# Output projection to MLP: the scheduler's order replaced by one written out by hand

## The chip, the core and the metric

The kernel runs on one core of a Trainium2 chip. TensorE (PE in the rows; its weight loads are PEld) multiplies matrices, VectorE (DVE), ScalarE (ACT) and GpSimd (POOL) do the work on elements, and SyncE (SP) issues the transfers from and to memory. Each engine has a queue of its own; semaphores order the engines among each other. The metric is the device time of one execution in microseconds (us), lower is better.

## What is computed

Two layers of a diffusion backbone, for 128 context tokens and 512 latent tokens that share the weights. The kernel keeps all 640 tokens in one array. Each layer ends so:

```python
merged = ga * (oa @ p['w_br_a']) + gb * (ob @ p['w_br_b']) + gc * (oc @ p['w_br_c'])
x = x + g1 * (merged @ p['w_out'])
h2 = _rmsnorm(x, p['norm2']) * (1 + sc2) + sh2
a, g = jnp.split(_dwconv3(h2 @ p['w_up'], p['conv_w'], p['conv_b']), 2, axis=-1)
x = x + g2 * ((jax.nn.silu(a) * g) @ p['w_down'])
```

`x` has 1024 channels, `w_out` is 1024 by 1024, `w_up` 1024 by 5632. `_rmsnorm` divides each token by the root of the mean of its squares over the 1024 channels. The change concerns the three lines in the middle: output projection, norm, first product of the MLP.

## The kernel before

Channels lie on the 128 partitions, tokens along the free axis. `x` is a tile of 128 x 8 x 640: eight channel blocks, 640 tokens. Every 32-bit operand is split into a high and a low part (`split`, L94: ScalarE writes the high part `hi` as a rounded copy, then VectorE the low part `lo` as the difference), and `mm3` (L111) makes a product of three matmuls: low weight by high data, high weight by low data, high by high. In the rows these three stand at L112, L113, L114.

A weight tile is fetched by `load_w` (L98): a transfer into `st` (three buffers), then the split into `wh` by ScalarE and `wl` by VectorE (five buffers of each). Splitting the weights is thus steady work for both engines during every dense stage.

The stretch in question begins at the end of `merge_phase` (L747), which leaves eight tiles `m32[n]`. `out_phase` (L816) splits them into `mh`/`ml` for the two token chunks `CH_B` (tokens 0 to 319 and 320 to 639). Then, for each chunk:

- eight output tiles, n = 0 to 7, of 24 matmuls each (eight channel blocks, three products) in the PSUM tile `wo`; after each, VectorE adds it to `x` with the gate (L837), ScalarE squares the new `x` into `sq` (L165) and the squares are summed in `acc` (class `Acc`: VectorE copies the first and adds the last, GpSimd adds those between);
- `bcast_rstd` (L173) and `rstd_bcast` (L182): TensorE sums `acc` over the partitions (`stat`), VectorE and GpSimd make the reciprocal roots in two pieces (128-wide and 64-wide), VectorE writes three diagonal tiles `dg` and TensorE spreads them over the partitions (`bc2`);
- `modulate` (L200): for each of the eight channel blocks and each token group (the first chunk holds 128 context and 192 latent tokens with different scales, the second only latent ones) VectorE writes `ht`, ScalarE `h2h`, VectorE `h2l`.

`mlp_up` (L848) then makes one `up` tile of `w_up` after another: 24 matmuls on the first chunk and 24 on the second into the two banks of one PSUM tile. There are three such double-bank tiles in PSUM; ScalarE reads each out twice (`u`, L861 and `v`, L862) before it comes free. The 44 `up` tiles of a layer alternate between the two halves of `w_up`.

The order of all this is not that of the code: the kernel is built with a scheduler that gives each engine's instructions an order by its own model of the time, over the whole program. In the program before, it lets `wo` tiles overlap, makes the modulation of the first chunk run between the additions of the second, and takes three `up` tiles through the first chunk before any goes to the second.

Of the kernel before, what the change touches and what calls it, by code (L numbers as in the profile page):

```python
# [27 lines left out]
F_T = 22  # L28
EPS = 1e-6
# [11 lines left out]
CH_B = [(0, 320), (320, 640)]  # L41
# [15 lines left out]
def trunk_kernel(ctx: ExitStack, tc: tile.TileContext, a: dict):  # L57
    nc = tc.nc
    dma = nc.sync.dma_start
    vec, act, pool, pe = nc.vector, nc.scalar, nc.gpsimd, nc.tensor  # L60
# [50 lines left out]
    def mm3(out, sh, sl, mh, ml, start, stop):  # L111
        pe.matmul(out, sl, mh, start=start, stop=False)  # L112
        pe.matmul(out, sh, ml, start=False, stop=False)  # L113
        pe.matmul(out, sh, mh, start=False, stop=stop)  # L114

    def powr(out, x):
        n = x.shape[1]
        pool.tensor_tensor(out=out, in0=x, in1=mhalf[:, :n], op=ALU.pow)
# [54 lines left out]
    def bcast_rstd(pl, sq, w, scale, ps):  # L173

        n = (w + P - 1) // P
        st = ps_t.tile([P, 8], F32, tag="p", name="stat")
        for j in range(n):
            m = min(P, w - j * P)
            pe.matmul(st[:m, j:j + 1], sq[:, j * P:j * P + m], ones[:, 0:1], start=True, stop=True)
        rstd_bcast(pl, st, w, scale, ps)  # L180
# [19 lines left out]
    def modulate(pl, x, bc, A, B, a0, b0, hi, lo):  # L200

        for s, e, j in _segs(a0, b0):
            r = slice(s - a0, e - a0)
            for k in range(ND):
                t = pl.tile([P, 320], F32, tag="ht", name="ht", bufs=3)[:, :e - s]
                vec.scalar_tensor_tensor(out=t, in0=x[:, k, s:e], scalar=A[:, k, j:j + 1], in1=bc[:, r],
                                         op0=ALU.mult, op1=ALU.mult)
                act.activation(hi[:, k, r], t, AF.Identity, bias=B[:, k, j:j + 1])  # L208
                vec.scalar_tensor_tensor(out=lo[:, k, r], in0=t, scalar=B[:, k, j:j + 1],  # L209
                                         in1=hi[:, k, r].bitcast(F32), op0=ALU.add, op1=ALU.subtract)  # L210
# [605 lines left out]
    def out_phase(l, x, rp, m32, hp, ps_d):  # L816

        mh = [hp.tile([P, 8, 320], F32R, tag=f"h{c}", name=f"mh{c}") for c in range(2)]
        ml = [hp.tile([P, 8, 320], F32R, tag=f"l{c}", name=f"ml{c}") for c in range(2)]
        for c, (a0, b0) in enumerate(CH_B):  # L820
            for n in range(8):
                split(m32[n][:, a0:b0], mh[c][:, n], ml[c][:, n], (vec, pool)[c])
        A2 = scale_cols(l, V_N2, 32, "A2")
        B2 = mods[l][:, 24:32, :]
        h2h, h2l = [], []
        for c, (a0, b0) in enumerate(CH_B):
            acc = Acc(rp, 320)
            for n0 in range(0, 8, 2):
                ps = ps_d.tile("wo")
                for j in range(2):  # L830
                    n = n0 + j
                    hi, lo = load_w(a["w_out"][l, n], 1024)
                    for k in range(ND):
                        ks = slice(k * P, (k + 1) * P)
                        mm3(ps[:, j, :320], hi[:, ks], lo[:, ks], mh[c][:, k], ml[c][:, k], k == 0, k == 7)
                    for s, e, jj in _segs(a0, b0):
                        vec.scalar_tensor_tensor(out=x[:, n, s:e], in0=ps[:, j, s - a0:e - a0],  # L837
                                                 scalar=mods[l][:, 16 + n, jj:jj + 1], in1=x[:, n, s:e],
                                                 op0=ALU.mult, op1=ALU.add)
                    acc.add(x[:, n, a0:b0], n == 7)  # L840
            h2h.append(hp.tile([P, 8, 320], F32R, tag=f"h{c}", name=f"h2h{c}"))
            h2l.append(hp.tile([P, 8, 320], F32R, tag=f"l{c}", name=f"h2l{c}"))
            bc = ps_t.tile([P, 512], F32, tag="p", name="bc2")
            bcast_rstd(rp, acc.acc, 320, 1.0 / D, bc)
            modulate(rp, x, bc, A2, B2, a0, b0, h2h[c], h2l[c])
        return h2h, h2l

    def mlp_up(l, f, h2h, h2l, mp, ps_d):  # L848
        vs = []
        for part in range(2):  # L850
            n = part * F_T + f
            hi, lo = load_w(a["w_up"][l, n], 1024)
            ps = ps_d.tile("up")
            for c in range(2):
                for k in range(ND):
                    ks = slice(k * P, (k + 1) * P)
                    mm3(ps[:, c, :320], hi[:, ks], lo[:, ks], h2h[c][:, k], h2l[c][:, k], k == 0, k == 7)
            u = mp.tile([P, T], F32, tag="u", name="u", bufs=2)
            v = mp.tile([P, T], F32, tag="v", name="v", bufs=4)
            cw = [vecs[l][:, V_CW + i * 44 + n:V_CW + i * 44 + n + 1] for i in range(3)]  # L860
            act.activation(u.rearrange("p (c n) -> p c n", c=2), ps[:, :, :320], AF.Copy)  # L861
            act.activation(v.rearrange("p (c n) -> p c n", c=2), ps[:, :, :320], AF.Identity,  # L862
                           bias=vecs[l][:, V_CB + n:V_CB + n + 1], scale=cw[1])
            for s, e in ((0, NP), (NP, T)):
                vec.scalar_tensor_tensor(out=v[:, s + 1:e], in0=u[:, s:e - 1], scalar=cw[0], in1=v[:, s + 1:e],  # L865
                                         op0=ALU.mult, op1=ALU.add)
                vec.scalar_tensor_tensor(out=v[:, s:e - 1], in0=u[:, s + 1:e], scalar=cw[2], in1=v[:, s:e - 1],
                                         op0=ALU.mult, op1=ALU.add)
            vs.append(v)
        va, vg = vs  # L870
        after[0] = vg[:, 0:1]
        act.activation(va, va, AF.Silu)
        vec.tensor_tensor(out=va, in0=va, in1=vg, op=ALU.mult)
        ah = mp.tile([P, T], F32R, tag="ah", name="ah", bufs=8)
        al = mp.tile([P, T], F32R, tag="al", name="al", bufs=8)
        split(va, ah, al)
        return ah, al
# [58 lines left out]
    def h0(a0, b0):  # L936

        j = 0 if a0 < NP else 1
        for k in range(ND):
            t = rp.tile([P, 320], F32, tag="ht", name="ht", bufs=3)[:, :b0 - a0]  # L940
            xs, hi = x[:, k, a0:b0], hh[:, k, a0:b0]
            act.activation(hi, xs, AF.Identity, bias=mods[0][:, k, j:j + 1], scale=A1[:, k, j:j + 1])
            vec.tensor_scalar(out=t, in0=xs, scalar1=A1[:, k, j:j + 1], scalar2=mods[0][:, k, j:j + 1],
                              op0=ALU.mult, op1=ALU.add)
            vec.tensor_tensor(out=hl[:, k, a0:b0], in0=t, in1=hi.bitcast(F32), op=ALU.subtract)
# [26 lines left out]
    for l in range(L):  # L972
# [11 lines left out]
        with ExitStack() as ms:  # L984
            mp = tp("mg", 1, ms)
            cs = modp.tile([P, 2, 1024], F32, tag="cs", name="cs", bufs=1)
            msteps = mod_steps(l, range(2, 6), modp, cs)
            m32 = merge_phase(l, x, cs, hh, hl, mp, ps_d, msteps)
            hst.close()
            hst = ExitStack()  # L990
            hp = tp("h2p", 1, hst, side="right")
            h2h, h2l = out_phase(l, x, rp, m32, hp, ps_d)
        with ExitStack() as ms:
            mp = tp("mlp", 1, ms)
            ups = {}
# [166 lines left out]
```

## Time and profile before

| | us |
|---|---|
| median of three runs | 2300.72 (2298.7 to 2303.47) |
| the profiled execution | 2307.55 |
| its span, first to last instruction | 2305.3 |
| layer 0: first `wo` matmul to first matmul of the fourth `up` tile | 639.65 to 727.05 |
| layer 1: the same | 1769.25 to 1856.66 |

The profiled execution is 6.8 us above the median. Times in rows count from the first instruction; one row is one instruction or several alike in a run (x2, x3). "idle before" is how long the engine had nothing to do, and after the arrow stands what ended it.

### The profile page before, as it was taken

To read this page: it belongs to the slowest core of one execution; us is meant where nothing else is said; L and a number is where in the kernel's file an instruction comes from. 1 tells how busy PE (TensorE), PEld (TensorE's weight loads), DVE (VectorE), ACT (ScalarE), POOL (GpSimd) and SP (SyncE) were. 2 spreads that over 40 slices of the span, in tenths; PEclk is the share of its full clock that TensorE was granted. 3 is DMA by queue.
4 is the path that set the end of the run, shared out by engine and by line. 5 is a ranking of instruction groups with operands and counts; after the bars stand their busy time and mean duration, and the time that the engine had idled before them with its cause. 6 is when DMAs were issued, how large, how long until landed. Compare 5 with 4: busy or idle time off the path is not lost. (4 is left out here: it accounts for less than half of the span.)

```text
span 2305.3 us, 37922 instructions
## 1 busy us (share of the span) xinstructions
PE 2225.9 (97%) x14778; PEld 2163.6 (94%) x14778; DVE 1562.8 (68%) x2913; ACT 975.7 (42%) x1728; POOL 528.4 (23%) x651
## 2 busy tenths in 40 slices
PE   8898999999999999999979999999999999999999
PEld 4898989989999999999969989899999999999999
DVE  6877687559567756765587867864895676554555
ACT  4555555432244423333355645653323453242422
POOL 3753443024041000000047533320422200000000
PEclk8999999999999999999999999999999999999999
DMA  7211223367333333432242112224762332322123
GB/s 256 80 57 59 82 66 107 108 244 228 121 121 106 101 104 121 135 102 88 75 128 83 57 49 83 97 89 135 283 210 89 123 110 92 94 65 90 50 84 114
DMA packets 102775, 258.50 MB, mean 112 GB/s; under 512 B 19523, under 2 KB 32579, under 8 KB 102596
## 3 DMA queue, kind: packets, MB, share of 16 engines
q1 hardware_dynamic: 102596, 256.09, 34.1%
q8 instruction: 116, 1.90, 0.3%
q14 instruction: 63, 0.51, 0.1%
HBM read 233.10 MB, written 22.95 MB: 111 GB/s over the span
## 5 line engine op out<-in xcount | busy, mean ns | idle before, releaser
L95 ACT ACTIVATE wh<-st 128x1024 fp32r<-128x1024 f32 (+3 forms) x336 | 314.7, 943 | 297.0 <-PE dn L114 170.8
L113 PE MATMUL up<-h2l,wh 128*128 128x320 f32 x1408 | 435.6, 310 | 2.5 <-DVE h2l L209 2.4
L112 PE MATMUL up<-h2h,wl 128*128 128x320 f32 x1408 | 433.5, 310 | 2.4 <-ACT v L862 1.4
L114 PE MATMUL up<-h2h,wh 128*128 128x320 f32 x1408 | 435.0, 310 | 0.0
L96 DVE TENSOR_TENSOR wl<-st,wh 128x1024 fp32r<-128x1024 f32 (+3 forms) x336 | 375.4, 1120 | 71.7 <-ACT wh L95 71.1
L113 PEld LDWEIGHTS up<-h2l,wh 128*128 128x128 f32 x1408 | 265.2, 189 | 3.6 <-DVE h2l L209 3.6
L112 PEld LDWEIGHTS up<-h2h,wl 128*128 128x128 f32 x1408 | 264.5, 189 | 4.0 <-ACT h2h L208 2.1
L114 PEld LDWEIGHTS up<-h2h,wh 128*128 128x128 f32 x1408 | 265.3, 189 | 0.1
L143 DVE SCALAR_TENSOR_TENSOR junk<-stm,cs 128x1024 bf16<-128x1024 f32 x172 | 223.2, 1298 | 60.1 <-DMA stm<-in_w_mod 57.2
L865 DVE SCALAR_TENSOR_TENSOR v<-u,vecs,v 128x127 f32<-128x127 f32 (+1 forms) x176 | 89.1, 547 | 183.4 <-ACT v L862 183.4
L112 PE MATMUL mm<-wh,hl 128*128 128x384 f32 x480 | 169.5, 353 | 15.0 <-ACT raw L361 10.8
L113 PE MATMUL dn<-al,wh 128*128 128x320 f32 x544 | 168.1, 309 | 0.0
L114 PE MATMUL dn<-ah,wh 128*128 128x320 f32 x544 | 168.1, 309 | 0.0
L112 PE MATMUL dn<-ah,wl 128*128 128x320 f32 x544 | 168.1, 309 | 0.0
L113 PE MATMUL mm<-wl,hh 128*128 128x384 f32 x480 | 163.7, 341 | 2.6 <-DVE wl L96 2.6
L114 PE MATMUL mm<-wh,hh 128*128 128x384 f32 x480 | 163.4, 340 | 0.0
L114 PE MATMUL gp<-hh,wh 128*128 128x320 f32 x480 | 148.6, 310 | 0.0
L112 PE MATMUL gp<-hh,wl 128*128 128x320 f32 x480 | 148.4, 310 | 0.0
L113 PE MATMUL gp<-hl,wh 128*128 128x320 f32 x480 | 148.3, 309 | 0.0
L112 PE MATMUL mmu<-hh,wl 128*128 128x384 f32 (+1 forms) x416 | 134.0, 322 | 4.0 <-ACT up L677 2.0
L114 PE MATMUL mmu<-hh,wh 128*128 128x384 f32 (+1 forms) x416 | 131.0, 315 | 0.0
L113 PE MATMUL mmu<-hl,wh 128*128 128x384 f32 (+1 forms) x416 | 130.4, 314 | 0.0
(226 smaller groups left out, 5444.6 us busy)
## 6 DMA issues: line engine op xcount, KB each, us to landing
stm<-in_w_mod SPq DMA_DIRECT2D x88, 512.0 KB, 4.3
st<-in_w_up SPq DMA_DIRECT2D x88, 512.0 KB, 3.6
st<-in_w_gate SPq DMA_DIRECT2D x48, 512.0 KB, 4.4
st<-in_w_unit SPq DMA_DIRECT2D x48, 384.0 KB, 3.2
st<-in_w_out SPq DMA_DIRECT2D x32, 512.0 KB, 3.6
st<-in_w_down SPq DMA_DIRECT2D x48, 320.0 KB, 3.0
st<-in_w_br SPq DMA_DIRECT2D x24, 512.0 KB, 3.6
st<-in_w_down SPq DMA_DIRECT2D x32, 384.0 KB, 3.2
```

Source lines behind the costliest of these rows:

```text
L95: act.activation(hi, x, AF.Copy)
L96: eng.tensor_tensor(out=lo, in0=x, in1=hi.bitcast(F32), op=ALU.subtract)
L112: pe.matmul(out, sl, mh, start=start, stop=False)
L113: pe.matmul(out, sh, ml, start=False, stop=False)
L114: pe.matmul(out, sh, mh, start=False, stop=stop)
L143: vec.scalar_tensor_tensor(out=junk, in0=st, scalar=1.0, in1=cs[:, j], op0=ALU.mult, op1=ALU.mult, accum_out=col)
L865: vec.scalar_tensor_tensor(out=v[:, s + 1:e], in0=u[:, s:e - 1], scalar=cw[0], in1=v[:, s + 1:e], op0=ALU.mult, op1=ALU.add)
```

## The change

The scheduler's order for this stretch is replaced: `out_phase` calls a new function `wo_up` inside a section in which each engine keeps the order of the code. Outside it the scheduler works as before.

What the hand-written order does:

- The sixteen `wo` tiles (i = 0 to 15, eight for each chunk) go through TensorE one after another, each complete. After the matmuls of tile i the code issues the load and split of weight tile i + 2, and after that the addition and the square of tile i. The three first `up` weight tiles are numbers 16, 17 and 18.
- The first square of a chunk is written straight into `acc`, with no copy. The sums `stat` are made in three 128-wide pieces at token offsets 0, 128 and 192, so one instruction each makes the mean, the reciprocal root and the diagonals (`dg3`, three at a time), and two matmuls of 256 and 64 columns spread them.
- The sums of the first chunk come after tile 8, their spread after tile 9. Its modulation goes in pieces of one channel block: one piece for each even tile from 10 on, two for each odd one, between the split of weight tile i + 2 and the addition of tile i. The low part of a block comes one piece later than its high part.
- Three `up` tiles then go through the first chunk. The sums of the second chunk stand between the first and the second of them, the spread within the third. The modulation of the second chunk is issued whole, and TensorE takes the three tiles through the second chunk block by block.
- `mlp_up` takes these three from `first` and makes only their readout; `ht` buffers grow from 320 to 384 columns.

```diff
-        for c, (a0, b0) in enumerate(CH_B):
-            acc = Acc(rp, 320)
-            for n0 in range(0, 8, 2):
...
+        with tc.manual_schedule():
+            wo_up(l, x, rp, mh, ml, hp, ps_d, A2, B2, h2h, h2l, first)
...
+            if n == 0:
+                accs.append(rp.tile([P, 384], F32, tag="acc", name="acc", bufs=1))
+                act.activation(accs[c][:, :320], x[:, n, a0:b0], AF.Square)
+                return
...
+        def diag(c):
+            dgs[c] = rp.tile([P, 3, P], F32, tag="ht", name="dg3", bufs=3)
+            vec.tensor_tensor(out=dgs[c], in0=ident.unsqueeze(1).to_broadcast([P, 3, P]),
+                              in1=rrs[c][:, :3].unsqueeze(2).to_broadcast([P, 3, P]), op=ALU.mult)
...
+        def pieces(c):
...
+            for k in range(ND):
+                t = rp.tile([P, 384], F32, tag="ht", name="ht", bufs=3)
...
+                if before is not None:
+                    low(*before)
+                before = k, t
+                yield
+            low(*before)
+            yield
...
+        for i in range(16):
+            c, n = divmod(i, 8)
+            if n % 2 == 0:
+                ps = ps_d.tile("wo")
+            hi, lo = W.pop(i)
+            for k in range(ND):
+                ks = slice(k * P, (k + 1) * P)
+                mm3(ps[:, n % 2, :320], hi[:, ks], lo[:, ks], mh[c][:, k], ml[c][:, k], k == 0, k == 7)
+            load(i + 2)
+            if i == 8:
+                last(0)
+                stat(0)
+            if i == 9:
+                diag(0)
+                spread(0)
+            if i >= 10:
+                p0 = p0 or pieces(0)
+                for _ in range(2 if i % 2 else 1):
+                    next(p0, None)
+            evac(i, ps)
+            if i == 8:
+                rstd(0)
+        u = [ps_d.tile("up")]
+        last(1)
+        for k in range(ND):
+            up(u[0], 16, 0, k)
+        load(18)
+        stat(1)
+        rstd(1)
+        diag(1)
...
+        for k in range(ND):
+            if k == 3:
+                spread(1)
+            up(u[2], 18, 0, k)
+        for _ in pieces(1):
+            pass
+        for k in range(ND):
+            for i in range(3):
+                up(u[i], 16 + i, 1, k)
```

The next rows are TensorE's in layer 0, in the first output tiles: `wo_7190` and `wo_7262` are the PSUM tiles of n = 0 and n = 1 in the program before, `mh0`, `ml0` the split input of the first chunk, whose last channel blocks come from the last tiles of the merge.

```order
L114 MATMUL wo_7190<-mh0_7152,wh_7193 128x320
L112 MATMUL wo_7262<-mh0_7152,wl_7266 128x320
L112 MATMUL wo_7190<-mh0_7152,wl_7194 128x320
L113 MATMUL wo_7262<-ml0_7154,wh_7265 128x320
L114 MATMUL wo_7262<-mh0_7152,wh_7265 128x320
L112 MATMUL wo_7262<-mh0_7152,wl_7266 128x320
L113 MATMUL wo_7262<-ml0_7154,wh_7265 128x320
```

In the changed program the same place reads so; `wo_7204` holds n = 0 and then n = 1 (weights `wh_7194`, then `wh_7200`).

```order
L112 MATMUL wo_7204<-mh0_7152,wl_7195 128x320
L113 MATMUL wo_7204<-ml0_7154,wh_7194 128x320
L114 MATMUL wo_7204<-mh0_7152,wh_7194 128x320
L112 MATMUL wo_7204<-mh0_7152,wl_7201 128x320
L113 MATMUL wo_7204<-ml0_7154,wh_7200 128x320
```

Before, tile n = 1 begins while n = 0 still lacks its last blocks; now n = 0 runs through all eight blocks first.

VectorE before, in the modulation of the first chunk (x is the addition of a `wo` tile, `wl_7899` and `wl_7962` are low parts of weight tiles):

```order
L206 SCALAR_TENSOR_TENSOR ht_7505<-x_5272,A2_7188,bc2_7477 128x128
L837 SCALAR_TENSOR_TENSOR x_5272<-wo_7631,mod0_88,x_5272 128x320
L209 SCALAR_TENSOR_TENSOR h2l0_7476<-ht_7497,mod0_88,h2h0_7475 128x128
L837 SCALAR_TENSOR_TENSOR x_5272<-wo_7700,mod0_88,x_5272 128x320
L209 SCALAR_TENSOR_TENSOR h2l0_7476<-ht_7501,mod0_88,h2h0_7475 128x128
L206 SCALAR_TENSOR_TENSOR ht_7509<-x_5272,A2_7188,bc2_7477 128x128
L96 TENSOR_TENSOR wl_7899<-st_7896,wh_7898 128x1024
L206 SCALAR_TENSOR_TENSOR ht_7513<-x_5272,A2_7188,bc2_7477 128x128
L209 SCALAR_TENSOR_TENSOR h2l0_7476<-ht_7505,mod0_88,h2h0_7475 128x128
L96 TENSOR_TENSOR wl_7962<-st_7959,wh_7961 128x1024
```

VectorE in the changed program, from the low part of weight tile 13 to that of weight tile 14 (`wo_7568` holds tiles 10 and 11; the addition here is that of tile 11):

```order
L96 TENSOR_TENSOR wl_7637<-st_7634,wh_7636 128x1024
L914 SCALAR_TENSOR_TENSOR ht_7640<-x_5272,A2_7188,bc2_7561 128x128
L914 SCALAR_TENSOR_TENSOR ht_7640<-x_5272,A2_7188,bc2_7561 128x192
L907 SCALAR_TENSOR_TENSOR h2l0_7600<-ht_7601,mod0_88,h2h0_7599 128x128
L907 SCALAR_TENSOR_TENSOR h2l0_7600<-ht_7601,mod0_88,h2h0_7599 128x192
L914 SCALAR_TENSOR_TENSOR ht_7647<-x_5272,A2_7188,bc2_7561 128x128
L914 SCALAR_TENSOR_TENSOR ht_7647<-x_5272,A2_7188,bc2_7561 128x192
L907 SCALAR_TENSOR_TENSOR h2l0_7600<-ht_7640,mod0_88,h2h0_7599 128x128
L907 SCALAR_TENSOR_TENSOR h2l0_7600<-ht_7640,mod0_88,h2h0_7599 128x192
L850 SCALAR_TENSOR_TENSOR x_5272<-wo_7568,mod0_88,x_5272 128x320
L96 TENSOR_TENSOR wl_7686<-st_7683,wh_7685 128x1024
```

Two whole channel blocks stand between a weight's low part and the addition, and the addition directly ahead of the next weight's low part.

ScalarE before, over the same stretch (`wh` is a weight's high part, `sq` the square of a new x tile, `h2h0` the high part of the modulated input):

```order
L165 ACTIVATE sq_7663<-x_5272 128x320
L208 ACTIVATE h2h0_7475<-ht_7497,mod0_88 128x128
L208 ACTIVATE h2h0_7475<-ht_7501,mod0_88 128x128
L95 ACTIVATE wh_7898<-st_7896 128x1024
L208 ACTIVATE h2h0_7475<-ht_7505,mod0_88 128x128
L95 ACTIVATE wh_7961<-st_7959 128x1024
L165 ACTIVATE sq_7697<-x_5272 128x320
L165 ACTIVATE sq_7732<-x_5272 128x320
```

ScalarE in the changed program, from the square of tile 10 to the high part of weight tile 14:

```order
L858 ACTIVATE sq_7607<-x_5272 128x320
L95 ACTIVATE wh_7636<-st_7634 128x1024
L918 ACTIVATE h2h0_7599<-ht_7640,mod0_88 128x128
L918 ACTIVATE h2h0_7599<-ht_7640,mod0_88 128x192
L918 ACTIVATE h2h0_7599<-ht_7647,mod0_88 128x128
L918 ACTIVATE h2h0_7599<-ht_7647,mod0_88 128x192
L858 ACTIVATE sq_7655<-x_5272 128x320
L95 ACTIVATE wh_7685<-st_7683 128x1024
```

Every weight's high part now stands directly behind the square of the tile three numbers earlier. Of the rest of the program the order stays, but for the attention of layer 1: there the scheduler, which sees other times ahead, interleaves the same instructions in another order over a stretch of about 1,150 matmul rows.

## Rows read from the trace of the kernel before

**Rows 1.** The page, part 1, TensorE: busy us (share) and instructions.

```profile
PE 2225.9 (97%) x14778; PEld 2163.6 (94%) x14778; DVE 1562.8 (68%) x2913; ACT 975.7 (42%) x1728; POOL 528.4 (23%) x651
```

**Rows 2.** Timeline of TensorE, layer 0: start, us, what.

```profile
639.65 0.31 PE L112 MATMUL wo<-mh,wl 128*128 128x320 f32 x1
...
682.20 0.61 PE L198 MATMUL bc<-dg,ones 128*128 128x128 f32 x4
...
699.36 0.42 PE L113 MATMUL up<-h2l,wh 128*128 128x320 f32 x1 [1.18 <-DVE h2l L209]
...
702.42 0.24 PE L179 MATMUL stat<-ones,acc 128*128 128x1 f32 x1 [0.98 <-DVE acc L171]
...
715.19 0.42 PE L112 MATMUL up<-h2h,wl 128*128 128x320 f32 x1 [0.45 <-ACT h2h L208]
...
727.05 0.41 PE L112 MATMUL up<-h2h,wl 128*128 128x320 f32 x1 [0.69 <-ACT v L862]
```

**Rows 3.** Timeline of TensorE, layer 1.

```profile
1769.25 0.31 PE L112 MATMUL wo<-mh,wl 128*128 128x320 f32 x1
...
1856.66 0.41 PE L112 MATMUL up<-h2h,wl 128*128 128x320 f32 x1 [0.69 <-ACT v L862]
```

**Rows 4.** Timeline of ScalarE, layer 0.

```profile
650.33 0.46 ACT L165 ACTIVATE sq<-x 128x320 f32<-128x320 f32 x1
650.69 1.04 ACT L95 ACTIVATE wh<-st 128x1024 fp32r<-128x1024 f32 x1
...
664.49 1.06 ACT L95 ACTIVATE wh<-st 128x1024 fp32r<-128x1024 f32 x1 [2.10 <-PE wo L114]
...
668.01 1.06 ACT L95 ACTIVATE wh<-st 128x1024 fp32r<-128x1024 f32 x1 [2.10 <-PE wo L114]
...
681.31 0.47 ACT L165 ACTIVATE sq<-x 128x320 f32<-128x320 f32 x1 [0.93 <-DVE x L837]
```

**Rows 5.** Windows, by engine; PEclk is the granted clock.

```profile
core 0: us, PE busy (x) PEld busy (x) DVE busy (x) ACT busy (x) POOL busy (x), PEclk, DMA share, GB/s
698.00:701.00 3.00, 1.75 (x11) 1.31 (x10) 3.00 (x8) 2.12 (x5) 0.83 (x1) 1.00 0.62 187
704.00:707.00 3.00, 3.00 (x13) 3.00 (x13) 2.49 (x9) 1.31 (x4) 1.37 (x2) 0.50 0.21 86
```

**Rows 6.** Timeline of VectorE, end of the merge, layer 0.

```profile
638.96 1.68 DVE L96 TENSOR_TENSOR wl<-st,wh 128x1024 fp32r<-128x1024 f32 x1
...
642.38 1.21 DVE L96 TENSOR_TENSOR wl<-st,wh 128x1024 fp32r<-128x1024 f32 x1
...
645.54 0.55 DVE L96 TENSOR_TENSOR ml<-m,mh 128x320 fp32r<-128x320 f32 x1 [0.54 <-ACT mh L95]
```

**Rows 7.** Timeline of VectorE, additions, modulation, weights, layer 0.

```profile
665.59 1.23 DVE L96 TENSOR_TENSOR wl<-st,wh 128x1024 fp32r<-128x1024 f32 x1 [0.42 <-ACT wh L95]
...
680.68 0.54 DVE L837 SCALAR_TENSOR_TENSOR x<-wo,mod,x 128x320 f32<-128x320 f32 x1
...
692.46 0.33 DVE L206 SCALAR_TENSOR_TENSOR ht<-x,A,bc 128x128 f32<-128x128 f32 x1
692.71 0.34 DVE L209 SCALAR_TENSOR_TENSOR h2l<-ht,mod,h2h 128x128 fp32r<-128x128 f32 x1
...
699.69 1.05 DVE L206 SCALAR_TENSOR_TENSOR ht<-x,A,bc 128x192 f32<-128x192 f32 x3
700.66 1.21 DVE L96 TENSOR_TENSOR wl<-st,wh 128x1024 fp32r<-128x1024 f32 x1
701.80 0.48 DVE L171 TENSOR_TENSOR acc<-acc,sq 128x320 f32<-128x320 f32 x1
```

**Rows 8.** Window in the attention of layer 1.

```profile
1300.00:1350.00 50.00, 43.22 (x261) 40.49 (x260) 42.04 (x102) 25.84 (x63) 17.03 (x30) 0.90 0.17 56
```

**Rows 9.** Waits of TensorE, 1150 to 1560: us, times, longest.

```profile
PE mm L112 <- ACT raw L361: 6.3, 6, 4.1
```

More of the change, by code (lines that the diff above doesn't have):

```diff
@@ L204, in modulate @@
             for k in range(ND):
-                t = pl.tile([P, 320], F32, tag="ht", name="ht", bufs=3)[:, :e - s]
+                t = pl.tile([P, 384], F32, tag="ht", name="ht", bufs=3)[:, :e - s]
                 vec.scalar_tensor_tensor(out=t, in0=x[:, k, s:e], scalar=A[:, k, j:j + 1], in1=bc[:, r],
@@ L824, in out_phase @@
         B2 = mods[l][:, 24:32, :]
-        h2h, h2l = [], []
-        for c, (a0, b0) in enumerate(CH_B):
-            acc = Acc(rp, 320)
-            for n0 in range(0, 8, 2):
-                ps = ps_d.tile("wo")
[L830 to L845, printed above, removed]
@@ L846, in out_phase, with wo_up, load, evac @@
-        return h2h, h2l
-    def mlp_up(l, f, h2h, h2l, mp, ps_d):
+        h2h, h2l, first = [], [], {}
+        with tc.manual_schedule():
+            wo_up(l, x, rp, mh, ml, hp, ps_d, A2, B2, h2h, h2l, first)
+        return h2h, h2l, first
+    def wo_up(l, x, rp, mh, ml, hp, ps_d, A2, B2, h2h, h2l, first):
+        ups = [(0, 0), (1, 0), (0, 1)]
+        W = {}
+        def load(i):
+            if i < 16:
+                W[i] = load_w(a["w_out"][l, i % 8], 1024)
+            elif i < 19:
+                part, f = ups[i - 16]
+                W[i] = load_w(a["w_up"][l, part * F_T + f], 1024)
+        accs, lasts = [], []
+        def evac(i, ps):
+            c, n = divmod(i, 8)
+            a0, b0 = CH_B[c]
+            for s, e, jj in _segs(a0, b0):
+                vec.scalar_tensor_tensor(out=x[:, n, s:e], in0=ps[:, n % 2, s - a0:e - a0],
+                                         scalar=mods[l][:, 16 + n, jj:jj + 1], in1=x[:, n, s:e],
+                                         op0=ALU.mult, op1=ALU.add)
+            if n == 0:
+                accs.append(rp.tile([P, 384], F32, tag="acc", name="acc", bufs=1))
+                act.activation(accs[c][:, :320], x[:, n, a0:b0], AF.Square)
+                return
+            sq = rp.tile([P, 384], F32, tag="sq", name="sq", bufs=2)
+            act.activation(sq[:, :320], x[:, n, a0:b0], AF.Square)
+            if n < 7:
+                pool.tensor_tensor(out=accs[c][:, :320], in0=accs[c][:, :320], in1=sq[:, :320], op=ALU.add)
+            else:
+                lasts.append(sq)
+        def last(c):
+            vec.tensor_tensor(out=accs[c][:, :320], in0=accs[c][:, :320], in1=lasts[c][:, :320], op=ALU.add)
+        OFF = (0, 128, 192)
+        st = {}
+        def stat(c):
+            st[c] = ps_t.tile([P, 8], F32, tag="p", name="stat")
+            for j, o in enumerate(OFF):
+                pe.matmul(st[c][:, j:j + 1], accs[c][:, o:o + P], ones[:, 0:1], start=True, stop=True)
+        rrs, dgs, bcs = {}, {}, {}
+        def rstd(c):
+            ms = small.tile([P, 8], F32, tag="ms", name="ms")
+            rrs[c] = small.tile([P, 8], F32, tag="rr", name="rr")
+            vec.tensor_scalar(out=ms[:, :3], in0=st[c][:, :3], scalar1=1.0 / D, scalar2=EPS,
+                              op0=ALU.mult, op1=ALU.add)
+            powr(rrs[c][:, :3], ms[:, :3])
+        def diag(c):
+            dgs[c] = rp.tile([P, 3, P], F32, tag="ht", name="dg3", bufs=3)
+            vec.tensor_tensor(out=dgs[c], in0=ident.unsqueeze(1).to_broadcast([P, 3, P]),
+                              in1=rrs[c][:, :3].unsqueeze(2).to_broadcast([P, 3, P]), op=ALU.mult)
+        def spread(c):
+            bcs[c] = ps_t.tile([P, 512], F32, tag="p", name="bc2")
+            pe.matmul(bcs[c][:, :256], ones, dgs[c][:, :2].rearrange("p j n -> p (j n)"), start=True, stop=True)
+            pe.matmul(bcs[c][:, 256:320], ones, dgs[c][:, 2, 64:], start=True, stop=True)
+        def pieces(c):
+            a0, b0 = CH_B[c]
+            hi = hp.tile([P, 8, 320], F32R, tag=f"h{c}", name=f"h2h{c}")
+            lo = hp.tile([P, 8, 320], F32R, tag=f"l{c}", name=f"h2l{c}")
+            h2h.append(hi)
+            h2l.append(lo)
+            before = None
+            def low(k, t):
+                for s, e, j in _segs(a0, b0):
+                    r = slice(s - a0, e - a0)
+                    vec.scalar_tensor_tensor(out=lo[:, k, r], in0=t[:, r], scalar=B2[:, k, j:j + 1],
+                                             in1=hi[:, k, r].bitcast(F32), op0=ALU.add, op1=ALU.subtract)
+            for k in range(ND):
+                t = rp.tile([P, 384], F32, tag="ht", name="ht", bufs=3)
+                for s, e, j in _segs(a0, b0):
+                    r = slice(s - a0, e - a0)
+                    vec.scalar_tensor_tensor(out=t[:, r], in0=x[:, k, s:e], scalar=A2[:, k, j:j + 1],
+                                             in1=bcs[c][:, r], op0=ALU.mult, op1=ALU.mult)
+                for s, e, j in _segs(a0, b0):
+                    r = slice(s - a0, e - a0)
+                    act.activation(hi[:, k, r], t[:, r], AF.Identity, bias=B2[:, k, j:j + 1])
+                if before is not None:
[4 more added lines that the diff above has]
+            yield
+        def up(ps, i, c, k):
+            hi, lo = W[i]
+            ks = slice(k * P, (k + 1) * P)
+            mm3(ps[:, c, :320], hi[:, ks], lo[:, ks], h2h[c][:, k], h2l[c][:, k], k == 0, k == 7)
+        load(0)
+        load(1)
+        p0 = None
+        for i in range(16):
+            c, n = divmod(i, 8)
+            if n % 2 == 0:
+                ps = ps_d.tile("wo")
+            hi, lo = W.pop(i)
+            for k in range(ND):
+                ks = slice(k * P, (k + 1) * P)
+                mm3(ps[:, n % 2, :320], hi[:, ks], lo[:, ks], mh[c][:, k], ml[c][:, k], k == 0, k == 7)
[21 more added lines that the diff above has]
+        diag(1)
+        u.append(ps_d.tile("up"))
+        for k in range(ND):
+            up(u[1], 17, 0, k)
+        u.append(ps_d.tile("up"))
+        for k in range(ND):
[4 more added lines that the diff above has]
+            pass
+        for k in range(ND):
+            for i in range(3):
+                up(u[i], 16 + i, 1, k)
+        first.update(zip(ups, u))
@@ L849, in mlp_up @@
+    def mlp_up(l, f, h2h, h2l, first, mp, ps_d):
         vs = []
@@ L851, in mlp_up @@
             n = part * F_T + f
[L852 to L857, printed above, removed]
+            ps = first.pop((part, f), None)
+            if ps is None:
+                hi, lo = load_w(a["w_up"][l, n], 1024)
+                ps = ps_d.tile("up")
+                for c in range(2):
+                    for k in range(ND):
+                        ks = slice(k * P, (k + 1) * P)
+                        mm3(ps[:, c, :320], hi[:, ks], lo[:, ks], h2h[c][:, k], h2l[c][:, k], k == 0, k == 7)
             u = mp.tile([P, T], F32, tag="u", name="u", bufs=2)
@@ L939, in h0 @@
         for k in range(ND):
-            t = rp.tile([P, 320], F32, tag="ht", name="ht", bufs=3)[:, :b0 - a0]
+            t = rp.tile([P, 384], F32, tag="ht", name="ht", bufs=3)[:, :b0 - a0]
             xs, hi = x[:, k, a0:b0], hh[:, k, a0:b0]
@@ L991, in trunk_kernel @@
             hp = tp("h2p", 1, hst, side="right")
-            h2h, h2l = out_phase(l, x, rp, m32, hp, ps_d)
+            h2h, h2l, first = out_phase(l, x, rp, m32, hp, ps_d)
         with ExitStack() as ms:
@@ L1000, in up_to @@
                 for i in range(len(ups), f):
-                    ups[i] = mlp_up(l, i, h2h, h2l, mp, ps_d)
+                    ups[i] = mlp_up(l, i, h2h, h2l, first, mp, ps_d)
                     for _ in range(1 if i < GROUPS[0][1] + 2 else 2):
```

## The prediction

> **What bounds the kernel now.** I read the page first: TensorE is busy 97% of the span [rows 1]. So the stretch can only gain where TensorE waits, runs at half clock or does small matmuls, and it loses whatever new wait the order puts in front of it. Then I read TensorE's timeline from the first `wo` matmul to the first matmul of the fourth `up` tile, which the edit does not own but which must follow it: 639.65 to 727.05, 87.40 us in layer 0, and 1769.25 to 1856.66, 87.41, in layer 1 [rows 2, 3]. The layers agree, so one sum serves both.
>
> What would it be without waits? ScalarE begins successive weight tiles at 664.49 and 668.01, both released by the end of a `wo` tile [rows 4]: TensorE takes 3.52 us for a tile of 24 matmuls, 0.1467 us each. The stretch has 16 `wo` tiles and three `up` tiles of two halves, 22 × 3.52 = 77.44 us. The excess is 9.96 us a layer. The timeline gives 1.18 (low part of the modulated input), 0.98 (`acc` for the sums), 0.45 (high part) and 0.69 (PSUM of the fourth `up` tile) as waits, 3.30 together [rows 2]. [...]
>
> Third, the queues. VectorE is busy all 3.00 us of 698 to 701, while TensorE has 1.75 [rows 5]. What it does there and when it may do it decides this change.
>
> **The change, part by part.** I follow VectorE, since in the new order its queue has one fixed loop from tile 10 on: low part of a weight (`wl`), one or two modulation pieces, addition of a tile (`x`), next `wl`.
>
> *The loop.* `wl` of tile i + 3 needs `wh` of that tile, which stands on ScalarE directly behind the square of tile i, which needs the addition of tile i. The rows price this chain: addition to square 0.63 (680.68 on VectorE, 681.31 on ScalarE), square to the next `wh` 0.36 (650.33 to 650.69), `wh` to `wl` 1.10 (664.49 to 665.59) [rows 4, 7]. That is 2.09 us from addition to `wl`, of which VectorE works only some 0.5. `wl` itself holds the queue 1.14 (700.66 to 701.80). A piece for one channel block is `ht` 0.25 (128 wide, 692.46 to 692.71), 0.32 (192 wide, a third of 699.69 to 700.66), and the two low parts, which I estimate 0.03 to 0.05 above those, 0.30 and 0.35: 1.22 us [rows 7]. One turn is then 2.09 + 1.14 + 1.22 = 4.45 with one piece and 5.67 with two. TensorE wants 3.52. Without the 1.5 us in which VectorE stands idle a turn, two turns would be 2 × 1.14 + 2 × 0.55 + 3 × 1.22 = 7.0 against TensorE's 7.04: the work fits, the order doesn't.
>
> Counted from the addition of tile 10, those of 11 to 15 come at 5.7, 10.1, 15.8, 20.2 and 25.3 us (in the last turn the low part of the seventh block stands in place of a piece's first half). TensorE ends tile 15 about 17.4 us after that addition. `wo` tiles don't stop for it, since their weights run two ahead and their PSUM tile is three pairs back; the delay comes out at the end of them:
> - `wl` of tile 16, the first `up`, ends at 15.76 + 2.09 + 1.14 + 0.06 = 19.05: TensorE waits 1.65.
> - The low part of the seventh channel block ends at 24.64. TensorE would need it 17.4 + 1.65 + 19 × 0.1467 = 21.84: it waits 2.8, and 0.1 for the eighth.
> - The sums of chunk 1 need the square of tile 15 and the addition to `acc` (25.3 + 0.63 + 0.47 + 0.48 = 26.9 [rows 4, 7]). TensorE is there five matmuls after the eighth block, at 25.5: it waits 1.3, about as in 702.42.
>
> *Merge end and first tile.* The new order runs tile 0 alone through all eight blocks. The last low part of the last block was ready at 645.54 + 0.55; the two weight splits ahead of it, 1.68 and 1.21 [rows 6], now stand elsewhere, so I put it at 643.2 to 643.8. TensorE is at it after 22 matmuls, 639.65 + 3.23 = 642.9. Wait between 0.3 and 0.9, or 3.2 if the splits stay ahead; I take 0.9 since part of the work before the split is unchanged.
>
> *Sums and spread of chunk 0.* From the end of tile 7, addition, square, `wh`, `wl`, addition to `acc` are 0.63 + 0.36 + 1.10 + 1.14 + 0.48 = 3.71, against one `wo` tile less 0.2, 3.32: 0.4 to 0.5 wait. The three sums take 0.78 and the spread about 0.6, the price of four spread matmuls in the row at 682.20 (0.61) [rows 2]; what was several instructions on other engines is fewer now. The wide diagonal shows in no row of before; from below it costs nothing extra, hidden behind `wo` tile 9, from above it takes 1.21 as a whole `wl` does and delays TensorE 0.5. I take nothing: it writes 384 columns, much nearer to the `acc` row's 320 (0.48) than to 1024. The second chunk pays the same 0.78 and 0.6.
>
> *The rest.* Modulation of chunk 1 is issued whole behind the spread in the third `up` tile: 15 matmuls, 2.2 us, cover it, against some 1.85 for the first block's spread to high part. It costs nothing there; if that cover is gone it costs 0.45, as at 715.19 [rows 2]. PSUM of the fourth tile stays a wait, 0.85 (0.69 and the spacing). The copy that opens `acc`, saved, was VectorE's and off the path: nothing. The weights' transfers go out in the same order, at a DMA share of 0.62 where it is busiest here [rows 5]: nothing. Seven stops cost 0.1 each for a slower first matmul: 0.7.
>
> [...]
>
> Sum a layer: 0.9 + 0.5 + 1.65 + 2.9 + 1.3 + 0.85 (waits, 8.1) + 1.56 + 1.2 (small matmuls) + 0.7 + 1.1 = 12.66; 77.44 + 12.66 = 90.1 against 87.4. Two layers: +5.4 us. The profiled execution took 2307.55, 6.8 above the median of the runs shown, so it would be 2313; on the median's scale I forecast 2300.7 + 5.4 = **2306.1**.
>
> [...]
>
> **Rivals.**
> - *R1, no half clock.* With the same waits the clock stays up: 1.1 less a layer, +3.2 in all, 2303.9. For it: the rows of before show one such drop a stretch, not its rule. Against: the waits are longer.
> - *R2, the clock stays low for long.* In 1300 to 1350, where TensorE has many short waits, the granted clock averages 0.90 [rows 8]: 50 × 0.10 = 5.0 us at full speed missing. If the three waits cost that instead of 1.1: 2306.1 + 2 × 3.9 = 2313.9. [...]
> - *R3, the order keeps pace (faster).* If the chain of 2.09 is much shorter than its single rows, because the addition, square and `wh` overlap more than the latencies tell, a turn comes to 3.52 and the waits of 1.65, 2.9, 1.3, 0.5, 0.4 of the first tile and the clock's 1.1 are gone: 7.85 less, 82.25 a layer, 2300.7 − 10.3 = 2290.4. It decides from a chain of about 1.55 down: five turns × 0.54 take 2.7 off the last addition, which brings back the time of before. For it: the work alone fits (7.0 in 7.04). Against: three rows of the chain, each without another wait between.
> - *R4, attention of layer 1.* Some 1,150 matmul rows there come in another order. Waits in that stretch reach 4.1 us one by one [rows 9]; one more or less of these moves the whole by 4.1: 2302 or 2310.
>
> **How the numbers follow.** Main case 0.40, with its own range 2302 to 2310 (first tile 0.3 to 3.2, diagonal 0 to 0.5, the cover of 0.45, low parts 0.25 to 0.35, twice); R1 0.15, R2 0.15, R3 0.20, R4 0.10. A measurement of this kernel tells about 0.2% from no change, 4.6 us: faster is below 2296.1, slower above 2305.3. Slower: 0.23 of the main case, 0.04 of R1, all of R2, half of R4 = 0.47. Faster: 0.18 of R3 and 0.01 of the main case = 0.19. The rest, 0.34, is no difference. The range runs from R3's value to R2's, 2290 to 2314, which leaves out about half of each of these two, 0.17.
>
> **What would show it.** In the changed profile: VectorE idle ahead of `wl`, released by `wh`, about 1.5 us in each turn from tile 10 on; additions of `wo` 4.4 and 5.7 us apart; TensorE waiting for `wl` of the first `up` tile (1.65), for `h2l` (2.8), for `acc` (1.3); a clock of 0.50 near the first `up` tile; 90.1 from first `wo` to fourth `up`. If additions follow each other at 3.5 us, R3 holds and I am wrong by sign. If the stretch comes out at 90 and the total does not, look at layer 1's attention or at what follows the fourth tile.

## The result: slower by 0.57%, and the profile after

The changed kernel took 2313.72 us (median of four, 2311.66 to 2317.2) against 2301.04 for the kernel before: a ratio of 1.0057, 95% interval 1.0039 to 1.0074, or 9 to 17 us more, 13 in the middle. Forecast were 5.4 more. The direction was right, the size less than half, and the place of the loss was wrong.

The page of the changed kernel: TensorE is busy for about the same time as in [rows 1], in a span that is longer, so the time went into waits. (The two profiled spans are only 7.1 us apart, since the profiled execution of before lies 6.8 above its median; the stretches below are the better measure.)

```profile
span 2312.4 us, 37875 instructions
PE 2223.0 (96%) x14770; PEld 2160.9 (93%) x14770; DVE 1557.8 (67%) x2897; ACT 978.6 (42%) x1728; POOL 513.5 (22%) x647
```

TensorE's timeline of the same kernel shows where: first layer 0, to set beside [rows 2], then the first and last row of layer 1, to set beside [rows 3], and between them its last stop.

```profile
636.21 0.31 PE L112 MATMUL wo<-mh,wl 128*128 128x320 f32 x1
...
639.85 0.42 PE L113 MATMUL wo<-ml,wh 128*128 128x320 f32 x1 [0.17 <-DVE ml L96]
640.10 0.31 PE L114 MATMUL wo<-mh,wh 128*128 128x320 f32 x1
...
641.18 0.42 PE L112 MATMUL wo<-mh,wl 128*128 128x320 f32 x1 [0.77 <-DVE x L850]
...
649.25 0.41 PE L112 MATMUL wo<-mh,wl 128*128 128x320 f32 x1 [0.77 <-DVE x L850]
...
657.33 0.42 PE L112 MATMUL wo<-mh,wl 128*128 128x320 f32 x1 [0.77 <-DVE x L850]
...
665.41 0.41 PE L112 MATMUL wo<-mh,wl 128*128 128x320 f32 x1 [0.77 <-DVE x L850]
...
673.14 0.83 PE L874 MATMUL stat<-ones,acc 128*128 128x1 f32 x6 [0.43 <-DVE acc L865]
...
682.42 0.41 PE L112 MATMUL wo<-mh,wl 128*128 128x320 f32 x1 [0.64 <-DVE x L850]
...
692.42 0.41 PE L112 MATMUL wo<-mh,wl 128*128 128x320 f32 x1 [2.70 <-DVE x L850]
...
702.42 0.41 PE L112 MATMUL wo<-mh,wl 128*128 128x320 f32 x1 [2.69 <-DVE x L850]
...
729.36 0.41 PE L112 MATMUL up<-h2h,wl 128*128 128x320 f32 x1 [0.69 <-ACT v L995]
...
1770.28 0.31 PE L112 MATMUL wo<-mh,wl 128*128 128x320 f32 x1
...
1836.87 0.41 PE L112 MATMUL wo<-mh,wl 128*128 128x320 f32 x1 [1.54 <-DVE x L850]
...
1863.78 0.41 PE L112 MATMUL up<-h2h,wl 128*128 128x320 f32 x1 [0.69 <-ACT v L995]
```

From the first `wo` matmul to the fourth `up` tile it is 93.15 us in layer 0 and 93.50 in layer 1, where it was 87.40 and 87.41: 11.8 us more in the two stretches together, inside the interval of the whole. Seven of the ten waits are a kind that the kernel before didn't have and the prediction didn't name: TensorE waits for an addition `x` (L850) before it may start a `wo` tile. They come once in a pair of tiles, at the start of tiles 1, 3, 5, 7 and 11, 13, 15 (ahead of tile 9 stand the sums of the first chunk, which cover it). The first is at 641.18, the start of tile 1: it waits 0.77 for the addition of tile 0, which ended just before. Tiles 0 and 1 are two halves of one PSUM tile, and the second half isn't begun until VectorE has read the first. From 640.10, the last matmul of tile 0, it is 1.08 us to the next matmul, not 0.147. So a pair takes 8.07 or 8.08 us (641.18 to 649.25, 649.25 to 657.33) where two tiles of 3.52 take 7.04: 1.03 us a stop. In the second chunk a pair takes 10.00 (682.42, 692.42, 702.42): 2.96 a stop.

What makes these longer is seen on VectorE around the stop at 692.42, which waits for the addition of 691.82; the loop is the one that the prediction priced.

```profile
687.40 0.55 DVE L850 SCALAR_TENSOR_TENSOR x<-wo,mod,x 128x320 f32<-128x320 f32 x1
689.50 1.23 DVE L96 TENSOR_TENSOR wl<-st,wh 128x1024 fp32r<-128x1024 f32 x1 [1.55 <-ACT wh L95]
...
691.82 0.55 DVE L850 SCALAR_TENSOR_TENSOR x<-wo,mod,x 128x320 f32<-128x320 f32 x1
693.91 1.23 DVE L96 TENSOR_TENSOR wl<-st,wh 128x1024 fp32r<-128x1024 f32 x1 [1.55 <-ACT wh L95]
...
697.40 0.55 DVE L850 SCALAR_TENSOR_TENSOR x<-wo,mod,x 128x320 f32<-128x320 f32 x1
```

From addition to `wl` it is 2.10 us (2.09 forecast), of which VectorE waits 1.55 for ScalarE's high part; the turns are 4.42 and 5.58 (4.45 and 5.67 forecast). A pair of 10.00 is the sum of two such turns. ScalarE's timeline holds the other half of the chain: square, then the weight's high part, behind the addition of 687.40.

```profile
688.05 0.47 ACT L858 ACTIVATE sq<-x 128x320 f32<-128x320 f32 x1 [0.66 <-DVE x L850]
688.42 1.05 ACT L95 ACTIVATE wh<-st 128x1024 fp32r<-128x1024 f32 x1
```

The clock, in windows of the changed kernel: three around the long stops of layer 1 and, last, the whole stretch of layer 0.

```profile
core 0: us, PE busy (x) PEld busy (x) DVE busy (x) ACT busy (x) POOL busy (x), PEclk, DMA share, GB/s
1820.00:1830.00 10.00, 7.30 (x42) 7.04 (x42) 6.91 (x18) 5.19 (x11) 1.76 (x2) 0.88 0.35 105
1828.00:1830.00 2.00, 2.00 (x9) 2.00 (x8) 2.00 (x5) 0.50 (x2) 0.01 (x1) 0.50 0.00 0
1830.00:1840.00 10.00, 8.46 (x54) 8.20 (x54) 6.61 (x16) 4.81 (x10) 1.77 (x2) 0.95 0.31 107
636.00:729.00 93.00, 82.97 (x551) 80.19 (x549) 53.58 (x100) 37.53 (x63) 18.50 (x20) 1.00 0.34 102
```

Layer 0 keeps the full clock (1.00) through all its stops. Layer 1 falls to the half clock for a while: in windows of one us it is 1.00 from 1820 to 1827, then 0.81, 0.50 from 1828 to 1831, and 0.99 or 1.00 from there to 1840, and 0.88 and 0.95 are the averages of these. 12% and 5% of 10 us are 1.7 us of full speed missing, but the next stop is shorter for it, 1.54 instead of 2.69, and the whole stretch is only 0.35 longer than that of layer 0.

**A sentence ahead of the prediction has to be corrected.** `wo_7262` in the order of the kernel before is called the PSUM tile of n = 1 there. It is that of n = 2, and later n = 3; n = 1 comes into `wo_7190`, after n = 0. TensorE's order before takes, in layer 0, 24 matmuls of each of `wo_7190`, `wo_7262` and `wo_7333` interleaved (n = 0, 2, 4), and then 24 more of each, one after the other (n = 1, 3, 5). In the rest of the stretch, too, another tile always stands between the two, so the scheduler's order never put the two halves of a PSUM tile one behind the other here. That is what the hand-written order gave up, and what the wrong reading hid.

### The profile page after: what moved, and what is told of

The parts are those of the page before. It is cut to its first block, busy times and chain, and to the rows that moved or that the text cites. A ratio compares the mean times of both kernels' runs of the same rounds, so it can differ in the third digit from the quotient of the medians.

```text
span 2312.4 us, 37875 instructions
## 1 busy us (share of the span) xinstructions
PE 2223.0 (96%) x14770; PEld 2160.9 (93%) x14770; DVE 1557.8 (67%) x2897; ACT 978.6 (42%) x1728; POOL 513.5 (22%) x647
```

## Experiments

The theory, T1: the second tile of a pair stops until the first has been added, because both lie in one PSUM tile; a stop costs 1.03 us in itself, and 2.96 where VectorE's loop has made the addition late. The rivals are named with the runs. All times below are medians beside runs of the kernel before on the same chip (2302.79 for the first four runs, 2301.91 for the other three).

**Own PSUM tiles.** The ring of three PSUM tiles turns with every `wo` tile; half of each stays unused.

```diff
-            if n % 2 == 0:
-                ps = ps_d.tile("wo")
+            ps = ps_d.tile("wo")
```

> Every wo tile takes a PSUM tile of its own in the ring of three, instead of two tiles sharing one; all else as in the change. Theory T1 (the second tile of a pair stops until VectorE has added the first, 1.04 us in chunk 0, up to 2.96 in chunk 1, because both lie in one PSUM tile): no stop on an addition is left, TensorE runs ahead in chunk 1 and the late VectorE loop comes out as the waits of the prediction, for wl of tile 16 (1.65), h2l (2.8), acc (1.3). A layer 88.3 to 89.4 instead of 93.3, total 2304 to 2306. Rival T2 (VectorE's loop alone sets the pace, the shared tile only shows where): stops of chunk 0 go, the time comes back in full at the end, a layer 92 or more, total 2311 or more.

2309.92 us, ratio 1.0037 (1.0025 to 1.0050). The stretch: 90.93 and 91.10 us a layer. TensorE's timeline in layer 0:

```profile
637.02 0.31 PE L112 MATMUL wo<-mh,wl 128*128 128x320 f32 x1
...
697.44 0.41 PE L112 MATMUL up<-h2h,wl 128*128 128x320 f32 x1 [1.40 <-DVE wl L96]
...
703.02 0.42 PE L113 MATMUL up<-h2l,wh 128*128 128x320 f32 x1 [2.53 <-DVE h2l L907]
...
705.32 1.41 PE L874 MATMUL stat<-ones,acc 128*128 128x1 f32 x6 [1.16 <-DVE acc L865]
...
727.95 0.41 PE L112 MATMUL up<-h2h,wl 128*128 128x320 f32 x1 [0.69 <-ACT v L994]
```

No wait for an addition is left. The lateness of VectorE's loop comes out at exactly the three places of the prediction: 1.40, 2.53 and 1.16 for 1.65, 2.8 and 1.3. The stretch and the total lie between those of T1 and those of T2. The gain is smaller than T1 expected, and the windows say why:

```profile
697.00:707.00 10.00, 5.88 (x31) 5.25 (x32) 7.40 (x17) 5.87 (x10) 0.88 (x1) 0.88 0.35 106
706.00:710.00 4.00, 4.00 (x17) 4.00 (x18) 3.25 (x5) 1.42 (x2) 1.76 (x1) 0.50 0.43 138
707.00:717.00 10.00, 10.00 (x56) 9.95 (x56) 5.02 (x9) 1.74 (x4) 1.76 (x1) 0.78 0.43 157
```

Behind these three waits, within 8 us, the granted clock stands at 0.50 from 706 to 710 and averages 0.88 and 0.78 in two stretches of 10 us: 3.4 us of full speed missing, in this layer and alike in layer 1 (0.89 and 0.77). Some of that falls into the wait for `acc`. What is lost can be read off: from the sums at 705.32 to the fourth `up` tile it is 22.63 us here, and 19.87 for the same instructions in the kernel with both edits (below, 697.88 to 717.75), about what they take at full clock: 120 matmuls 0.1467 us apart are 17.60, the sums 0.80, the spread some 0.6 and the last wait 0.85 (an estimate from these rows). The difference is 2.8 us, 1.7 more than the 1.1 that the prediction charged.

**Own PSUM tiles in the first chunk alone.**

```diff
-            if n % 2 == 0:
+            if n % 2 == 0 or c == 0:
                 ps = ps_d.tile("wo")
```

> Own PSUM tiles for the eight tiles of the first chunk only; in the second chunk pairs share as in the change. T1: the four stops of 1.04 us go and nothing takes their place, since VectorE's turn there (2.10 + 1.14) is shorter than TensorE's 3.52: 4.2 us less a layer, 89.1, total about 2305. T2: the additions of the second chunk come no earlier, total 2311 or more.

2307.98 us, ratio 1.0020 (1.0011 to 1.0029); 88.98 and 89.01 us a layer, 4.2 less than the change in layer 0, as T1 had it, and 4.5 in layer 1, where the change had the half clock besides. The four stops of the first chunk are gone, those of the second unchanged (its first, the row at 677.15, is the 0.64 of 682.42):

```profile
635.09 0.31 PE L112 MATMUL wo<-mh,wl 128*128 128x320 f32 x1
...
677.15 0.41 PE L112 MATMUL wo<-mh,wl 128*128 128x320 f32 x1 [0.64 <-DVE x L850]
...
724.07 0.42 PE L112 MATMUL up<-h2h,wl 128*128 128x320 f32 x1 [0.69 <-ACT v L995]
```

The first stop of the second chunk comes 42.06 us behind the first `wo` matmul, not 46.21: the additions there come earlier, which T2 denied. T2 falls, although the total lies between the two expectations. The clock stayed at 1.00 in it:

```profile
635.00:724.00 89.00, 81.79 (x550) 80.06 (x548) 53.44 (x100) 37.68 (x64) 18.43 (x19) 1.00 0.35 107
```

It is the clock that makes this kernel 2.0 us a layer shorter than the one with own tiles throughout: without the 2.8 us lost there, that one would be the shorter by some 0.8 (an estimate from the rows of both).

**High part early.** `load` is cut in two. ScalarE's part stands ahead of the square, VectorE's where the whole stood.

```diff
-            evac(i, ps)
+            high(i + 3)
+            evac(i, ps)
```

`high(i)` fetches weight tile i and makes `wh`; `load(i + 2)`, in its old place, now makes `wl` alone.

> Pairs share PSUM as in the change, but the high part of weight tile i + 3 stands on ScalarE ahead of the square of tile i, not behind it, so that VectorE's low part needn't wait for the addition. T1 with the loop as priced in the prediction: addition to wl falls from 2.10 to about 0.5, two turns from 10.0 to about 7.0, so the three stops of 2.96 in chunk 1 shrink to the 1.04 of a shared tile: 5.8 us less a layer, 87.5, total about 2302. Rival T3 (VectorE's work itself is the loop, or ScalarE becomes it): the pair stays near 10.0 us, total 2312 to 2315.

2302.15 us, ratio 1.0003 (0.9994 to 1.0012): this alone brings back the time of before. The stretch is 88.59 and 88.57, a layer 1.1 more than expected: the expectation shortened three stops of 2.96, but the change has only two such (692.42, 702.42); the first of its second chunk is 0.64. VectorE's timeline, and TensorE's, in layer 0:

```profile
688.87 0.55 DVE L860 SCALAR_TENSOR_TENSOR x<-wo,mod,x 128x320 f32<-128x320 f32 x1 [0.56 <-PE wo L114]
689.33 1.22 DVE L850 TENSOR_TENSOR wl<-st,wh 128x1024 fp32r<-128x1024 f32 x1
```

```profile
635.76 0.31 PE L112 MATMUL wo<-mh,wl 128*128 128x320 f32 x1
...
640.73 0.42 PE L112 MATMUL wo<-mh,wl 128*128 128x320 f32 x1 [0.77 <-DVE x L860]
...
689.47 0.41 PE L112 MATMUL wo<-mh,wl 128*128 128x320 f32 x1 [0.64 <-DVE x L860]
...
724.35 0.41 PE L112 MATMUL up<-h2h,wl 128*128 128x320 f32 x1 [0.69 <-ACT v L1008]
```

`wl` follows the addition after 0.46 us instead of 2.10, and VectorE now waits for TensorE (0.56), not the other way round. The bare stops of the pairs stay. T3 falls: VectorE's work fits.

**Both.**

> Both edits. T1: no stop on additions and the loop keeps pace with TensorE: 82.5 to 83.5 us a layer, total 2291 to 2294, faster than before by 7 to 10 us. T2 or T3: one of the two costs stays, total 2304 or more.

2289.47 us, ratio 0.9949 (0.9936 to 0.9961), faster than the kernel before; 81.95 and 81.94 us a layer, half a microsecond below what was expected. Of all the waits in TensorE's timeline, those of 0.2 at the merge's end and these two are left:

```profile
635.80 0.31 PE L112 MATMUL wo<-mh,wl 128*128 128x320 f32 x1
...
697.88 0.80 PE L884 MATMUL stat<-ones,acc 128*128 128x1 f32 x6 [0.23 <-DVE acc L875]
...
717.75 0.42 PE L112 MATMUL up<-h2h,wl 128*128 128x320 f32 x1 [0.69 <-ACT v L1007]
```

**Shared PSUM tiles in another turn.** With the high part early, pairs share PSUM as in the change, but the tiles go in the scheduler's manner.

```diff
+        TURN = (0, 2, 1, 3, 4, 6, 5, 7)
...
-            c, n = divmod(i, 8)
-            if n % 2 == 0:
-                ps = ps_d.tile("wo")
+            c, n = i // 8, TURN[i % 8]
+            if n % 2 == 0:
+                pss[n // 2] = ps_d.tile("wo")
+            ps = pss[n // 2]
```

> Pairs share a PSUM tile as in the change and the early high part is kept; the output tiles are taken in the order 0, 2, 1, 3, 4, 6, 5, 7, so that another tile lies between the two of a pair. T1 (the stop is the wait for the addition of the tile just ended, since it shares the PSUM tile): as with own PSUM tiles, about 82 us a layer instead of 88.6, total 2288 to 2292. Rival T4 (own PSUM tiles helped by the longer ring, eight tiles rather than four turns, or by what follows in the program): 85 us a layer or more, total 2295 or more.

2293.19 us, ratio 0.9958 (0.9946 to 0.9970), and 81.97 and 81.95 us a layer:

```profile
637.55 0.31 PE L112 MATMUL wo<-mh,wl 128*128 128x320 f32 x1
...
719.52 0.41 PE L112 MATMUL up<-h2h,wl 128*128 128x320 f32 x1 [0.69 <-ACT v L1011]
```

The stretch is the same to 0.02 us as with own tiles, so the seven stops come from the nearness of the two halves, not from how often the ring turns; T4 falls by the stretch. The stop is a wait that the program itself asks for: the first matmul of the second half is released by the addition (`x` in the rows; 0.77 at 641.18 in the change). Whether TensorE could write one half while VectorE reads the other, no run here tests. The two medians differ by more than the stretches, but their intervals overlap.

**The end of the first three up tiles.** Own tiles and early high part; the last two channel blocks tile by tile.

```diff
-        for k in range(ND):
-            for i in range(3):
-                up(u[i], 16 + i, 1, k)
+        for k in range(6):
+            for i in range(3):
+                up(u[i], 16 + i, 1, k)
+        for i in range(3):
+            for k in range(6, ND):
+                up(u[i], 16 + i, 1, k)
```

> Own PSUM tiles and early high part; the three up tiles go through the second chunk block by block only up to the sixth of eight blocks, and then finish one after the other, so that ScalarE reads the first out while the others still run. If the wait of 0.69 for the readout (about 0.9 with the slower restart) is the price of ending together, a layer takes 81.0 to 81.3 instead of 81.95, total 1.3 to 1.9 less than with both edits, 2287.5 to 2288.5. Rival: the low parts of the last blocks are not ready that early, TensorE waits for h2l instead and nothing is won.

2290.91 us, ratio 0.9957 (0.9945 to 0.9969).

```profile
633.13 0.31 PE L112 MATMUL wo<-mh,wl 128*128 128x320 f32 x1
...
714.22 0.38 PE L112 MATMUL up<-h2h,wl 128*128 128x320 f32 x1
```

The wait of 0.69 is gone from TensorE's list of waits, and from 633.13, the first `wo` matmul, to the fourth `up` tile at 714.22 it is 81.09 us, 0.86 less, as expected. The whole doesn't show it: 1.7 us in two layers are below what these runs tell (their six times lie between 2286.36 and 2294.95). So the step is shown in the stretch and left open in the total.

**Layer 0 alone.** Layer 1 runs the code of before.

```diff
-        with tc.manual_schedule():
-            wo_up(l, x, rp, mh, ml, hp, ps_d, A2, B2, h2h, h2l, first)
+        if l == 0:
+            with tc.manual_schedule():
+                wo_up(l, x, rp, mh, ml, hp, ps_d, A2, B2, h2h, h2l, first)
+        else:
+            for c, (a0, b0) in enumerate(CH_B):
...
```

> The change in layer 0 alone; layer 1 keeps the scheduler's order of before. If the loss lies in the two stretches alone (5.75 and 6.1 us in the traces), layer 0 takes 93.2, layer 1 87.4, and the total is 5 to 7 above before, 2307 to 2309. Rival R4 of the prediction (part of the 12.7 comes from the reordered attention of layer 1, or from a stretch outside): total more than 9 above or less than 4 above before.

2307.98 us, ratio 1.0025 (1.0013 to 1.0036). TensorE's timeline, and last a window of layer 0:

```profile
638.30 0.31 PE L112 MATMUL wo<-mh,wl 128*128 128x320 f32 x1
...
731.83 0.41 PE L112 MATMUL up<-h2h,wl 128*128 128x320 f32 x1 [0.69 <-ACT v L1017]
...
1771.52 0.31 PE L112 MATMUL wo<-mh,wl 128*128 128x320 f32 x1
...
1858.92 0.42 PE L112 MATMUL up<-h2h,wl 128*128 128x320 f32 x1 [0.69 <-ACT v L1017]
690.00:700.00 10.00, 7.32 (x40) 7.05 (x39) 6.61 (x17) 5.19 (x10) 1.75 (x2) 0.83 0.34 102
```

93.53 in layer 0, and 87.40 in layer 1, as in the kernel before. Here the half clock fell into layer 0 (0.83 from 690 to 700, where the matmuls from 695.82 to 699.02 start 0.267 us apart), which the change's own layer 0 didn't have: 0.4 more than its 93.15. One layer costs 6.1 us in the stretch and 6.1 in the medians (3.0 to 8.3 by the interval): the loss is additive and local.

## Why the prediction was right in sign and wrong in size

**The step that failed** stands in the part on the loop: "`wo` tiles don't stop for it, since their weights run two ahead and their PSUM tile is three pairs back". The ring of PSUM tiles is three long, but it counts from pair to pair. Within a pair the second tile writes into the PSUM tile that VectorE has still to read. The row at 641.18 shows the wait, own PSUM tiles and the other turn each take all of them away, and a lower end for its price stood in the rows: the addition's own 0.54 [rows 7]. The order listing of the change stood ahead of the prediction with "`wo_7204` holds n = 0 and then n = 1" in it; the argument read it for the first tile's blocks only.

**What that did to the sum**, a layer. The sum had 0 for the four stops of the first chunk; they cost 4.1 (the first chunk's own tiles took 4.2 off in layer 0). For the second chunk it had waits of 1.65, 2.9 and 1.3 behind the last `wo` tile, 5.85; they didn't come, since TensorE was held at the pairs instead, 0.9 + 2 × 2.96 = 6.8. So the loop's lateness was there in the expected size but in another place. The sum has 1.1 a layer for the half clock; no run shows that as the price of the three waits. In its place layer 0 of the change had none, layer 1 lost 0.35, and own PSUM tiles, with three such waits, 2.8. The first tile waited 0.17 of the 0.9 taken, below the lower end of 0.3. Balance: 90.1 + 4.1 + 6.8 − 5.85 − 1.1 − 0.7 = 93.35, against 93.15 and 93.50.

**The mechanism that was right** is VectorE's loop. Chain and turns are within 2% of the forecast, and putting the high part ahead of the square takes 4.6 and 4.9 us a layer off the change by itself. ScalarE keeps the written order in the trace: idle for 0.66 ahead of the square at 688.05, it starts the high part that stands behind it only at 688.42, though that weight's transfer, issued at 676.7, had landed long before (3.5 us from issue to landing), and `wl` waits 1.55 for it.

**The rivals.** R1, no half clock, held in layer 0 of the change (1.00 from 636 to 729). R2, a clock that stays low, didn't come in the change (0.50 for three us in layer 1); that its 2313.9 meets the measured 2313.72 is chance, since the time went into stops. Something like it came with own PSUM tiles: 2.8 us a layer lost, where R2 took 5.0. For the window at 0.50 in [rows 5], too, 1.1 is low: the 13 matmuls there count one that had begun before 704; the others of that window start 0.267 us apart instead of 0.1467, which loses 1.35 in the 3 us. With own PSUM tiles the prediction's whole sum can be tested, as that kernel has the PSUM that the prediction assumed: 90.9 and 91.1 against 90.1. The difference is the clock (+1.7) against the first tile and the three waits, shorter by some 0.8 together from matmul to matmul. R3, the order keeps pace, was refuted for this order, and is what both edits reach: 81.95 a layer against R3's 82.25, a ratio of 0.9949 against R3's 0.9955 (2290.4 of 2300.7). R4, the attention of layer 1, has no part in it, as far as one profiled execution of each tells: from the first `dl` matmul of layer 0 to the first `wo` matmul of layer 1 it is 633.8 us before, 632.5 in the change and 631.3 with the change in layer 0 alone. Only the profile of own tiles in the first chunk has 639.6 there; it is the slowest of that kernel's eleven runs. The total of the change in layer 0 alone says the same, 6.1 above before.

**Other steps.** Sums of the first chunk: 0.43 waited (0.4 to 0.5 forecast). The wide diagonal (0.55 for 384 columns, at 676.61) delayed nothing, neither did the second chunk's modulation, whose first up tile block by block had no wait. PSUM of the fourth `up` tile: 0.69, as before. A first matmul after a stop takes 0.41 or 0.42, and the next starts 0.25 behind it, not 0.147: 0.1 a stop, as the sum had it.

## What to carry to other kernels

Where an order is written by hand, list for each instruction not only what feeds it but what must have been read out of the buffer that it writes, and count the distance in instructions, not in buffers: here two halves of one PSUM tile counted as one buffer (0.77 of waiting between them, 2.70 where the addition came late). A scheduler's odd-looking turn (0, 2, 4, 1, 3, 5) may be what keeps that distance. And in a loop through engines that keep the written order, as ScalarE did here (0.66 idle ahead of the square, with the high part behind it), what prepares work for three tiles ahead must not stand behind what waits for the present one: moving one instruction ahead of the square won back about 4.7 of the 5.9 us a layer that the change had lost (means of the two layers).

## What the runs showed of the hardware that was not expected

Stops of 2.70 and 2.69 us, ten us apart, left the granted clock at 1.00 in layer 0; in layer 1 of the same execution the windows with the first of these and the next stop have 0.88 and 0.95. With the change in layer 0 alone it was layer 0 that fell, to 0.83 in the window with its first long stop. Three stops of 1.40, 2.53 and 1.16 within 8 us, with own PSUM tiles, gave 0.88 and 0.78 in layer 0, 0.89 and 0.77 in layer 1. So the lost time can't be read from the sum of the waits: 6.0 us in the second chunk of the change's layer 0 cost nothing of the clock, 5.1 with own PSUM tiles cost 2.8. What decides between 1.00 and 0.88 for the same stops, the runs leave open.
